# The output gate's vector-matrix product as running sums on VectorE, with TensorE adding over the partitions

## The chip, the cores and the metric

The kernel runs on one core of a Trainium2 chip. The metric is the device time of one launch, in microseconds, as the median of several runs. The engines are TensorE (PE, with PEld for its weight loads), VectorE (DVE), ScalarE (ACT), GpSimd (POOL) and SyncE (SP, which here only issues DMAs). Each engine works through its own list of instructions in a fixed order, and an instruction that waits holds up everything behind it on that engine.

## The reference

Two sequences, a prompt of 1024 tokens and a sample of 512, pass through one encoder layer with shared weights. A condition vector c (one for each sequence) gives three modulation vectors of 1024 through silu(c) @ w_ada + b_ada: shift, scale and the output gate. The layer is, cut to what matters:

```
def mod(c):  return split(silu(c) @ w_ada + b_ada, 3)     # shift, scale, gate: 1024 each
h   = rms_norm(x) * g * (1 + scale) + shift
p   = h @ w_in                                            # q, k, v, gate of both branches
o_r = bidirectional_retention(rope(q_r), rope(k_r), v_r)  # 4 heads of 128
o_a = blocked_gqa(rope(norm(q_a)), rope(norm(k_a)), v_a)  # 8 query heads, 2 key heads
y   = x + gate * (concat(o_r * silu(g_r), o_a * silu(g_a)) @ w_out)
```

The change touches one thing only: how the vector gate = silu(c) @ w_ada[:, 2048:3072] + b_ada[2048:3072] is computed for the two sequences, and where in the program that happens.

## The kernel before, in words

`sequence` runs twice: first for the sample (4 tiles of 128 tokens, first=True), then for the prompt (8 tiles). The first pass also makes shift and scale, loads and splits the weights, prepares w_out (`split_wo`) and computes the gate of both sequences. A float32 weight is split into a high and a low part (`split`: a cast on ACT, then a subtraction at line 139 on POOL for even quarters and on DVE for odd ones), and each product is three matmuls (`mm3`, lines 148 to 150).

For each retention head h the units of `head_units` project q and k (tile pqk), then v and gate (pvg). Into these, `weave` and `merge` put the steps of the head before (`ret_core`): states (psts, line 695, from vds and the rotated key ss), R0s and R1s, the decayed queries qd0s and qd1s (line 718), scores, the sum of squares sss, then m_rets and r_rets on POOL, the gated output mxs and its transpose pms. Rotation of q and k runs as rt1s (line 631) and rt2s (line 636) on DVE, and their sum ss (line 639) on POOL.

The gate comes from `gate_mod`, a generator with 16 steps. Each step loads a piece of w_ada, gr (two 128-row blocks by 256 columns, 256 KB, line 246), and issues two matmul calls with the condition vectors scT as weights (line 250, four records to a step), which add up in the PSUM banks pgm0 and pgm1. ACT copies them to gmod (line 253), and `load_gate` (line 391) adds the four column groups, the bias row and spreads the result over the partitions by a matmul with the table `sel`. `GSTEPS` says how many steps are woven into the units of heads 1, 2 and 3: 7, 7 and 3.

The pieces gr share a ring of four buffers (tag raw) with the raw quarters of all weights, for example wqks2r and wvgs2r; a DMA into the ring waits until the former content was read. The blocks of w_out (wor, line 177) go through POOL (woz, line 142), DVE (line 139) and a DMA back to HBM (wod, line 184), which POOL issues. The order of each engine's list is set by a scheduler from its own model of the times. In names, s stands for the sample, p for the prompt.

Of the kernel before, what the change touches and what calls it, by code (L numbers as in the profile page):

```python
# [11 lines left out]
F32 = mybir.dt.float32  # L12
# [3 lines left out]
ALU = mybir.AluOpType  # L16
# [3 lines left out]
P = 128  # L20
D = 1024
KD = D // P
# [22 lines left out]
def _shape_tables():  # L45
    f = np.float32
    m = np.arange(P, dtype=f)
    ident = np.eye(P, dtype=f)
    c, r = m[None, :], m[:, None]
    fwd = np.maximum(c - r, 0).astype(f)  # L50
    bwd = np.maximum(r - c, 0).astype(f)
    qf = np.broadcast_to(c + 1, (P, P))
    qb = np.broadcast_to(P - c, (P, P))
    kcol = np.ascontiguousarray(np.stack([P - 1 - m, m], 1).astype(f))
    geo = np.concatenate([fwd, bwd, qf, qb], 1).astype(f)
    sel = np.zeros((P, 2), f)
    for ct in range(4):
        for q in range(2):
            sel[32 * ct + q, q] = 1
    sel[2, :] = 1  # L60

    def rope(hd):
        half = hd // 2
        fr = (10000.0 ** (-np.arange(0, half, 2, dtype=f) / f(half))).astype(f)
        tok = np.arange(1024)
        row = (tok // GRID_W).astype(f)[:, None] * fr[None, :]
        col = (tok % GRID_W).astype(f)[:, None] * fr[None, :]
        cos = np.concatenate([np.cos(row)] * 2 + [np.cos(col)] * 2, 1)
        sin = np.concatenate([-np.sin(row), np.sin(row), -np.sin(col), np.sin(col)], 1)
        return [np.ascontiguousarray(a.astype(f).reshape(8, P, hd).transpose(1, 0, 2)) for a in (cos, sin)]  # L70

    rc, rs = rope(P)
    ac, as_ = rope(DH)
    return {"ident": ident, "geo": geo, "kcol": kcol, "sel": sel,
            "rope_rc": rc, "rope_rs": rs, "rope_ac": ac, "rope_as": as_}


# [1 line left out]
def hybrid_layer_kernel(ctx: ExitStack, tc: tile.TileContext, a: dict, y_prompt: bass.AP, y_sample: bass.AP):  # L79
    nc = tc.nc  # L80
    V, S, G, T = nc.vector, nc.scalar, nc.gpsimd, nc.tensor
# [3 lines left out]
    w_ada = a["w_ada"][0]  # L85
# [5 lines left out]
    cst = ctx.enter_context(pool("cst", bufs=1))  # L91
# [8 lines left out]
    def bank(name):  # L100
        return pcur[-1].tile([P, 512], F32, tag="bank", name=name)
# [6 lines left out]
    nc.sync.dma_start(staged, a["ident"])  # L108
    V.tensor_copy(identr, staged)
    ident = identr.bitcast(F32)  # L110
    sel = cst.tile([P, 2], F32, name="sel")
    nc.sync.dma_start(sel, a["sel"])
    mhalf = cst.tile([P, 16], F32, name="mhalf")
    V.memset(mhalf, -0.5)
    zo = cst.tile([P, 4, DH], F32R, name="zo")
# [3 lines left out]
    ones = zo[:, 2, :].bitcast(F32)  # L119
# [9 lines left out]
    scT = cst.tile([P, KD, 32], F32, name="scT")  # L129
# [5 lines left out]
    gmod = [cst.tile([P, 512], F32, name=f"gmod{n}") for n in range(2)]  # L135
# [8 lines left out]
    def ada_bias(row, c0):  # L144
        nc.sync.dma_start(row, a["b_ada"][:, c0 : c0 + 512])
# [90 lines left out]
                               op0=ALU.add, op1=ALU.add)  # L236
        V.tensor_tensor(aT[:, ks, :], md[:, n : 2 * n, :], bc(ngT[:, ks]), op=ALU.mult)

    def gate_mod(wring):
        for n in range(2):  # L240
            pm = bank(f"pgm{n}")
            for q in range(2):
                for qt in range(4):
                    raw = wring.tile([P, 2, 256], F32, tag="raw", name=f"gr{n}{q}{qt}", bufs=4)
                    c0 = 2 * D + n * 512 + q * 256
                    nc.sync.dma_start(raw, w_ada[qt * 256 : (qt + 1) * 256, c0 : c0 + 256].rearrange("(k p) c -> p k c", p=P))
                    for i in range(2):
                        k = qt * 2 + i
                        ct = k % 4
                        T.matmul(pm[32 * ct : 32 * ct + 32, q * 256 : (q + 1) * 256], scT[:, k, :], raw[:, i, :],  # L250
                                 start=(k < 4), stop=(k >= 4))
                    yield
            S.copy(gmod[n], pm)
            ada_bias(gmod[n][2:3, :], 2 * D + n * 512)

    def merge(p, n, q, m):
        done = 0
# [52 lines left out]
    def behind_ada():  # L310
        return tc.issue_after(adma[-1].ins)

    GSTEPS = {1: 7, 2: 7, 3: 3}

    def sequence(r, nt, first):
        tg = "ps"[r]
# [3 lines left out]
        with ExitStack() as sctx:  # L320
# [14 lines left out]
            kv = {}  # L335
# [52 lines left out]
            def load_gate():  # L388
                for n in range(2):
                    pgb = bank(f"pgb{tg}{n}")  # L390
                    T.matmul(pgb, sel[:, r : r + 1].broadcast_to([P, P]), gmod[n], start=True, stop=True)
                    S.copy(kv["gate"][n], pgb)

            wq = []
# [105 lines left out]
            with ExitStack() as rctx:  # L500
# [26 lines left out]
                if first:  # L527
                    with pool("st", bufs=1, reuse_waits="tile") as st:
# [8 lines left out]
                        ws, parts, i = [], [], 0  # L537
# [63 lines left out]
                def decay_tables():  # L601
                    S.activation(lg, lg, AF.Exp)
                    V.tensor_scalar_mul(lg, lg, -1.0)
                    S.activation(gd, lg, AF.Exp, scale=float(P))
                    V.memset(lns, math.log(RSCALE))
                    for h in range(RH):
                        V.tensor_scalar_mul(DT[:, h, :], geo[:, 0:P], lg[:, 0, h : h + 1])
                        V.scalar_tensor_tensor(out=DT[:, h, :], in0=geo[:, P : 2 * P], scalar=lg[:, 1, h : h + 1],
                                               in1=DT[:, h, :], op0=ALU.mult, op1=ALU.add)
                        for d in range(2):  # L610
                            S.activation(QD[:, d, h, :], geo[:, (2 + d) * P : (3 + d) * P], AF.Exp, scale=lg[:, d, h : h + 1])
                            S.activation(kd[:, d, h : h + 1], kcol[:, d : d + 1], AF.Exp, scale=lg[:, d, h : h + 1], bias=lns)
                    S.activation(DT, DT, AF.Exp, bias=lns)
# [177 lines left out]
                nsteps = 7 * ng + 1  # L791

                prev = None
                gsteps = gate_mod(wring) if first else None
                wctx = rctx.enter_context(ExitStack())
                wst = wctx.enter_context(pool(f"wst{tg}", bufs=2, reuse_waits="tile")) if first else None
                for h in range(RH + 1):
                    if h < RH:
                        sls = [slot(f"s{tg}{h}_{i}") for i in range(nt // 2)]
                        units, n = head_units(h, sls), 2 * nt  # L800
                    else:
                        wctx.close()
                        if first:
                            units, n = kvq_units(rctx.enter_context(pool(f"pa{tg}", bufs=2, reuse_waits="tile"))), 2 * nt
                        else:
                            units, n = gates(rp, "rt1"), 8 * ng
                    extra, m = itertools.islice(gsteps, GSTEPS.get(h, 0)) if first else iter(()), nsteps
                    if first:
                        m += GSTEPS.get(h, 0)
                    weave(units, n, merge(prev, nsteps, extra, m - nsteps), m + ((2, 3)[r] if h == RH else 0))  # L810
                    if h == 0:
                        decay_tables()
                    if first and h < RH:
                        for j in range(sum(WOH[:h]), sum(WOH[: h + 1])):
                            with tc.issue_after(acts["w"].ins):
                                split_wo(wst, j)
                    if h < RH:
                        prev = ret_core(h, sls)
# [318 lines left out]
```

## Time and profile before

| | |
|---|---|
| median of 3 runs (lowest, highest) | 989.43 us (989.29, 991.23) |
| span of the profiled execution | 985.3 us |
| TensorE matmul busy | 938.8 us (95%) |
| TensorE weight load busy | 813.9 us (83%) |
| VectorE busy | 626.1 us (64%) |
| ScalarE busy | 414.3 us (42%) |
| GpSimd busy | 507.7 us (52%) |

The profile is of one execution. Busy time is the time in which an engine ran an instruction. The span runs from the first to the last instruction; the measured time also has what lies around it. In a timeline each line is one instruction or several alike in a row: its start, how long it took, the engine, the line of the code, the operation, output <- inputs, shapes, and in square brackets how long the engine sat idle before it and what ended that.

### The profile page before, as it was taken

What the parts mean: (1) busy time and instruction counts of PE and PEld (TensorE: products, weight loads), DVE (VectorE), ACT (ScalarE), POOL (GpSimd) and SP (SyncE); (2) the same over time, 40 slices, a digit from 0 to 9 for tenths busy, and PEclk for the clock granted to TensorE, in tenths of its full rate; (3) what the DMA queues carried; (4) which work ended last, traced back from release to release, by engine and by line L of the source; (5) the groups of instructions that cost most, each with busy time, mean ns of one, the idle gap of its engine ahead of it and who ended that gap; (6) DMA issues with size and microseconds to landing.
All of it is one profiled execution on the core that took longest, in us unless ns stands there. A gap on an engine that the chain in (4) does not pass through costs nothing. (4 is left out here: it accounts for less than half of the span.)

```text
span 985.3 us, 15952 instructions
## 1 busy us (share of the span) xinstructions
PE 938.8 (95%) x6249; PEld 813.9 (83%) x6249; DVE 626.1 (64%) x1039; ACT 414.3 (42%) x656; POOL 507.7 (52%) x404
## 2 busy tenths in 40 slices
PE   4889998999999999999999999999979999999998
PEld 3779898987676799999999988999847776776776
DVE  2474556667886683534435243457988878978975
ACT  4252233353646652122321322241465655655562
POOL 4243544474647663122223012255899779777882
PEclk9999998999999999999999999999999999999999
DMA  9964876321911711111111112100071110111011
GB/s 274 275 191 144 269 225 218 87 78 57 382 67 44 239 50 47 41 43 44 44 35 28 26 43 70 47 7 12 1 296 68 43 44 1 44 43 45 20 43 44
DMA packets 95687, 93.02 MB, mean 94 GB/s; under 512 B 23502, under 2 KB 84858, under 8 KB 92540
## 3 DMA queue, kind: packets, MB, share of 16 engines
q1 hardware_dynamic: 92876, 77.85, 25.8%
q0 software_dynamic: 2736, 14.16, 3.6%
q8 instruction: 49, 0.80, 0.3%
q14 instruction: 26, 0.21, 0.1%
HBM read 77.30 MB, written 14.68 MB: 93 GB/s over the span
## 5 line engine op out<-in xcount | busy, mean ns | idle before, releaser
L924 POOL TENSOR_TENSOR qp<-qp,pp 128x512 f32<-128x512 f32 x96 | 159.5, 1661 | 21.3 <-ACT pp L912 15.3
L139 DVE TENSOR_TENSOR plp<-pp,php 128x1024 fp32r<-128x1024 f32 x64 | 93.6, 1464 | 19.8 <-ACT php L138 19.7
L912 ACT ACTIVATE pp<-pTp 128x1024 f32<-128x1024 f32 x64 | 65.6, 1025 | 76.8 <-PE pTp L909 40.7
L856 DVE TENSOR_REDUCE nmp<-pnp 128x1 f32<-128x1024 f32 x64 | 77.3, 1212 | 11.4 <-PE pnp L854 11.4
L138 ACT CAST php<-pp 128x1024 fp32r<-128x1024 f32 x64 | 67.2, 1051 | 16.2 <-PE pop L939 14.9
L148 PE MATMUL pvgp<-wvgp,hhp 128*128 128x256 f32 x224 | 65.1, 291 | 0.0
L148 PE MATMUL pqkp<-wqkp,hhp 128*128 128x256 f32 x224 | 64.7, 289 | 0.0
L149 PE MATMUL pvgp<-wvgp,hhp 128*128 128x256 f32 x224 | 64.4, 288 | 0.0
L150 PE MATMUL pvgp<-wvgp,hlp 128*128 128x256 f32 x224 | 63.9, 285 | 0.0
L150 PE MATMUL pqkp<-wqkp,hlp 128*128 128x256 f32 x224 | 63.7, 284 | 0.0
L149 PE MATMUL pqkp<-wqkp,hhp 128*128 128x256 f32 x224 | 63.4, 283 | 0.0
L940 PE MATMUL pop<-plp,VVp 128*128 128x512 f32 x128 | 52.1, 407 | 5.7 <-DVE plp L139 5.6
L148 PE MATMUL pyp<-wo,Mhp 128*128 128x512 f32 (+1 forms) x136 | 52.8, 389 | 1.2 <-DVE op L951 0.7
L150 PE MATMUL pyp<-wo,Mlp 128*128 128x512 f32 (+1 forms) x136 | 51.6, 382 | 0.5 <-DVE Mlp L139 0.5
L149 PE MATMUL pyp<-wo,Mhp 128*128 128x512 f32 (+1 forms) x136 | 51.9, 382 | 0.0
L639 POOL TENSOR_TENSOR sp<-rt1p,rt2p 128x512 f32<-128x512 f32 x16 | 22.5, 1405 | 56.4 <-DVE rt2p L636 56.4
L939 PE MATMUL pop<-php,VVp 128*128 128x512 f32 x128 | 51.0, 398 | 0.3 <-ACT php L138 0.3
L124 POOL TENSOR_SCALAR m_retp<-ssp 128x4 f32<-128x4 f32 x8 | 1.6, 195 | 89.6 <-DVE ssp L745 89.4
L897 PE MATMUL pTp<-Q1Tp,kkp 128*128 128x512 f32 x128 | 41.4, 404 | 3.6 <-ACT pp L912 2.9
L148 PEld LDWEIGHTS pqkp<-wqkp,hhp 128*128 128x128 f32 x224 | 43.0, 192 | 0.0
L149 PEld LDWEIGHTS pqkp<-wqkp,hhp 128*128 128x128 f32 x224 | 43.0, 192 | 0.0
L150 PEld LDWEIGHTS pqkp<-wqkp,hlp 128*128 128x128 f32 x224 | 42.9, 192 | 0.0
(465 smaller groups left out, 3120.7 us busy)
## 6 DMA issues: line engine op xcount, KB each, us to landing
wo<-wod SPq DMA_DIRECT2D x16, 1024.0 KB, 5.8
wa<-in_w_ada_dram SPq DMA_DIRECT2D x16, 512.0 KB, 6.4
wod<-woz POOLq DMA_DIRECT2D x8, 1024.0 KB, 6.0
gr<-in_w_ada_dram SPq DMA_DIRECT2D x16, 256.0 KB, 4.8
xn<-in_x_prompt_dram SPq DMA_DIRECT2D x8, 512.0 KB
xrp<-in_x_prompt_dram SPq DMA_DIRECT2D x8, 512.0 KB, 3.4
out_dram<-xrp POOLq DMA_DIRECT2D x7, 512.0 KB, 3.0
xs<-in_x_sample_dram SPq DMA_DIRECT2D x4, 512.0 KB, 6.1
```

The source lines that it names most:

```text
L138: hi_eng(hi, src)
L139: lo_eng.tensor_tensor(lo, src, hi.bitcast(F32), op=ALU.subtract)
L148: T.matmul(out, lh, rh, start=first, stop=False)
L149: T.matmul(out, lh, rl, start=False, stop=False)
L150: T.matmul(out, ll, rh, start=False, stop=last)
L639: G.tensor_tensor(qk, t1, t2, op=ALU.add)
L856: V.tensor_reduce(nm[:, h : h + 1], pn[:, :ntok], AX.X, ALU.max, negate=True)
L897: T.matmul(pT[:, i * 512 : (i + 1) * 512], kk[v][:, kb], st8[t]["Q1T"][:, hs, :].rearrange("p h q -> p (h q)"), start=True, stop=False)
L912: S.activation(p, pT, AF.Exp)
L924: G.tensor_tensor(acc, acc, p[:, i * 512 : (i + 1) * 512], op=ALU.add)
L939: T.matmul(po, lv, ph[:, c], start=(kb == 0), stop=False)
L940: T.matmul(po, lv, pl[:, c], start=False, stop=(kb == nt - 1))
```

## The change

`gate_mod` no longer uses TensorE. `gate_start`, called after head 0's units, clears four 128x512 accumulators with POOL (gmod0 and gmod1 for the prompt, the two tiles kv["gate"], called gates in the lists, for the sample) and loads the bias into their row 0 by four DMAs. Each of the 16 steps loads one 128-row block by 512 columns (again 256 KB) and runs two scalar_tensor_tensor instructions on DVE, one for each sequence: accumulator = block * scT + accumulator, with one scalar to a partition. That makes 32 instructions on 128x512 float32 with both inputs in SBUF. `load_gate` then adds over the 128 partitions with the same number of matmuls as before, with a column of ones in place of `sel`, whose table and load are gone. Head 3 gets 2 steps in place of 3.

```diff
-    def gate_mod(wring):
-        for n in range(2):
-            pm = bank(f"pgm{n}")
-            for q in range(2):
-                for qt in range(4):
-                    raw = wring.tile([P, 2, 256], F32, tag="raw", name=f"gr{n}{q}{qt}", bufs=4)
-                    c0 = 2 * D + n * 512 + q * 256
-                    nc.sync.dma_start(raw, w_ada[qt * 256 : (qt + 1) * 256, c0 : c0 + 256].rearrange("(k p) c -> p k c", p=P))
-                    for i in range(2):
-                        k = qt * 2 + i
-                        ct = k % 4
-                        T.matmul(pm[32 * ct : 32 * ct + 32, q * 256 : (q + 1) * 256], scT[:, k, :], raw[:, i, :],
-                                 start=(k < 4), stop=(k >= 4))
-                    yield
-            S.copy(gmod[n], pm)
-            ada_bias(gmod[n][2:3, :], 2 * D + n * 512)
+    def gate_start(accs):
+        for acc in accs:
+            for n in range(2):
+                G.memset(acc[n], 0.0)
+                ada_bias(acc[n][0:1, :], 2 * D + n * 512)
+
+    def gate_mod(wring, accs):
+        for k in range(KD):
+            for n in range(2):
+                raw = wring.tile([P, 512], F32, tag="raw", name=f"gr{n}{k}", bufs=4)
+                c0 = 2 * D + n * 512
+                nc.sync.dma_start(raw, w_ada[k * P : (k + 1) * P, c0 : c0 + 512])
+                for r, acc in enumerate(accs):
+                    V.scalar_tensor_tensor(out=acc[n], in0=raw, scalar=scT[:, k, r : r + 1], in1=acc[n], op0=ALU.mult, op1=ALU.add)
+                yield
...
-    GSTEPS = {1: 7, 2: 7, 3: 3}
+    GSTEPS = {1: 7, 2: 7, 3: 2}
...
-                    T.matmul(pgb, sel[:, r : r + 1].broadcast_to([P, P]), gmod[n], start=True, stop=True)
+                    T.matmul(pgb, ones[:, 0:1].broadcast_to([P, P]), kv["gate"][n], start=True, stop=True)
...
-                gsteps = gate_mod(wring) if first else None
+                gsteps = gate_mod(wring, (gmod, kv["gate"])) if first else None
...
+                        if first:
+                            gate_start((gmod, kv["gate"]))
```

The scheduler's lists differ in the stretch from about 20 to 200 us; behind it they are alike but for line numbers. In the lists below a name ends in the numbers of its buffer and its tile: gr00 is row block 0 of half 0 (the digits are half, then block).

DVE's list at the end of the last normalised tile (hls) and the first rotation of head 0 (rt1s, rt2s), before:

```order
L139 TENSOR_TENSOR wvgs1_840<-wvgs1r1_846,wvgs1_840 128x2x256
L511 TENSOR_SCALAR hfs0_7_542<-xTs0_7_536,aT_81,shT_80 128x512
L513 TENSOR_TENSOR hls0_98<-hfs0_7_542,hhs0_97 128x512
L139 TENSOR_TENSOR wvgs1_840<-wvgs1r3_856,wvgs1_840 128x2x256
L631 TENSOR_TENSOR rt1s0_0_762<-p0s0_0_186,rc_738 128x2x128 x2
L636 TENSOR_TENSOR rt2s0_0_763<-p0s0_0_186,rs_740 128x128 x4
```

The same place on DVE after:

```order
L132 TENSOR_TENSOR wvgs1_846<-wvgs1r1_852,wvgs1_846 128x2x256
L230 TENSOR_TENSOR aT_79<-md7_529,ngT_80 128x2
L503 TENSOR_SCALAR hfs0_7_540<-xTs0_7_534,aT_79,shT_78 128x512
L132 TENSOR_TENSOR wvgs1_846<-wvgs1r3_862,wvgs1_846 128x2x256
L505 TENSOR_TENSOR hls0_96<-hfs0_7_540,hhs0_95 128x512
L245 SCALAR_TENSOR_TENSOR gmod0_82<-gr00_897,scT_76,gmod0_82 128x512
L245 SCALAR_TENSOR_TENSOR gates0_109<-gr00_897,scT_76,gates0_109 128x512
L245 SCALAR_TENSOR_TENSOR gmod1_83<-gr10_944,scT_76,gmod1_83 128x512
L245 SCALAR_TENSOR_TENSOR gates1_110<-gr10_944,scT_76,gates1_110 128x512
L245 SCALAR_TENSOR_TENSOR gmod0_82<-gr01_980,scT_76,gmod0_82 128x512
L245 SCALAR_TENSOR_TENSOR gates0_109<-gr01_980,scT_76,gates0_109 128x512
L623 TENSOR_TENSOR rt1s0_0_760<-p0s0_0_184,rc_736 128x2x128 x2
```

Six of the new instructions, on three pieces, now stand ahead of the first rt1s, and two more stand between rt1s and rt2s.

POOL's list at the same time, from the last split of head 1's weights to the first rotated key (ss), before:

```order
L139 TENSOR_TENSOR wvgs1_840<-wvgs1r2_851,wvgs1_840 128x2x256 [waits DMAHW7_49,DMAHW0_49,Activation_49]
L639 TENSOR_TENSOR ss0_0_760<-rt1s0_0_762,rt2s0_0_763 128x512 [waits DVE_49,PE_49]
L142 TENSOR_SCALAR woz0_1191<-wor0_1189 128x2x512 [waits DMAHW1_49,DMAHW7_49,PE_49,Pool_49]
L639 TENSOR_TENSOR ss0_1_761<-rt1s0_1_771,rt2s0_1_772 128x512 [waits DVE_49]
L184 DMA wod0_60<-woz0_1191 128x2048 [waits DVE_49]
```

And after:

```order
L132 TENSOR_TENSOR wvgs1_846<-wvgs1r2_857,wvgs1_846 128x2x256 [waits DMAHW3_49,DMAHW2_49,Activation_49]
L135 TENSOR_SCALAR woz0_1196<-wor0_1194 128x2x512 [waits DMAHW4_49,PE_49,Pool_49]
L631 TENSOR_TENSOR ss0_0_758<-rt1s0_0_760,rt2s0_0_761 128x512 [waits DVE_49]
L177 DMA wod0_60<-woz0_1196 128x2048 [waits DVE_49]
L631 TENSOR_TENSOR ss0_1_759<-rt1s0_1_769,rt2s0_1_770 128x512 [waits DVE_49]
```

The block of w_out, which waits for a DMA, has changed places with the first ss. In SP's list the load of that block (wor0) stood behind four pieces gr before, and stands behind six after; the fifth and the sixth wait for a ring buffer that DVE's new instructions give back.

DVE's list at head 0's sum of squares and output, before:

```order
L362 SCALAR_TENSOR_TENSOR ss1_0_817<-tg_s1_0_1095,pvgs1_0_1034 128x256
L745 TENSOR_REDUCE sss0_0_1111<-sqs0_0_1109 128x4
L750 SCALAR_TENSOR_TENSOR mxs0_0_1117<-pos0_0_1098,r_rets0_0_1115,ss0_0_760 128x128 x2
L750 SCALAR_TENSOR_TENSOR mxs0_0_1117<-pos0_0_1098,r_rets0_0_1115,ss0_1_761 128x128 x2
L362 SCALAR_TENSOR_TENSOR ss1_1_818<-tg_s1_1_1180,pvgs1_1_1126 128x256
```

And after:

```order
L354 SCALAR_TENSOR_TENSOR ss1_0_823<-tg_s1_0_1100,pvgs1_0_1039 128x256
L132 TENSOR_TENSOR woz1_1573<-wor1_1571,woz1_1573 128x2x512
L132 TENSOR_TENSOR woz2_1580<-wor2_1577,woz2_1580 128x2x512
L737 TENSOR_REDUCE sss0_0_1116<-sqs0_0_1114 128x4
L742 SCALAR_TENSOR_TENSOR mxs0_0_1122<-pos0_0_1103,r_rets0_0_1120,ss0_0_758 128x128 x2
```

Two splits of w_out blocks now stand ahead of the sum of squares; on POOL their copies and both wod DMAs stand ahead of m_rets and r_rets in the same way. At head 1's sum of squares one such split (woz4) has moved ahead of mxs.

## Rows read from the trace of the kernel before

**Rows 1.** The page's first part: busy us, share of the span, instructions.

```profile
PE 938.8 (95%) x6249; PEld 813.9 (83%) x6249; DVE 626.1 (64%) x1039; ACT 414.3 (42%) x656; POOL 507.7 (52%) x404
```

**Rows 2.** All that touches tile gr: durations, then idle us and times, landing.

```profile
L250 PE MATMUL pgm<-gr,scT x64: 376/380/404, 65.9 to 143.9; 128*32 128x256 f32 x64
...
  DMA gr<-in_w_ada_dram: 6.4, 7
...
  PE pgm L250: 3.3, 4
...
DMA to landing us min/median/max: 2.7/4.8/7.8
```

**Rows 3.** Timeline of PE from 65 to 74 us.

```profile
65.66 0.27 PE L150 MATMUL pqks<-wqks,hls 128*128 128x256 f32 x1
65.87 0.63 PE L250 MATMUL pgm<-gr,scT 128*32 128x256 f32 x4
...
66.64 0.28 PE L149 MATMUL pqks<-wqks,hhs 128*128 128x256 f32 x1
...
69.28 0.28 PE L150 MATMUL pqks<-wqks,hls 128*128 128x256 f32 x1
...
71.37 0.63 PE L250 MATMUL pgm<-gr,scT 128*32 128x256 f32 x4 [0.83 <-DMA gr<-in_w_ada_dram]
73.00 0.63 PE L250 MATMUL pgm<-gr,scT 128*32 128x256 f32 x4 [1.00 <-DMA gr<-in_w_ada_dram]
73.55 0.71 PE L695 MATMUL psts<-vds,ss 128*128 128x128 f32 x4
```

**Rows 4.** Timeline of DVE from 60 to 69 us.

```profile
60.42 0.69 DVE L139 TENSOR_TENSOR wvgs<-wvgs1r,wvgs 128x512 fp32r<-128x512 f32 x1 [0.93 <-ACT wvgs L138]
...
62.02 1.48 DVE L513 TENSOR_TENSOR hls<-hfs,hhs 128x512 fp32r<-128x512 f32 x1
...
64.33 0.76 DVE L631 TENSOR_TENSOR rt1s<-p0s,rc 128x256 f32<-128x256 f32 x2 [0.23 <-PE p0s L150]
65.00 0.87 DVE L636 TENSOR_TENSOR rt2s<-p0s,rs 128x128 f32<-128x128 f32 x4
...
68.02 1.13 DVE L608 SCALAR_TENSOR_TENSOR DT<-geo,lg,DT 128x128 f32<-128x128 f32 x4
```

**Rows 5.** Timelines of DVE and of POOL at 351 us, in the prompt.

```profile
351.63 1.91 DVE L608 SCALAR_TENSOR_TENSOR DT<-geo,lg,DT 128x128 f32<-128x128 f32 x4
...
351.41 1.20 POOL L298 TENSOR_SCALAR xn<-xn,r_x 128x1024 f32<-128x1024 f32 x1
```

**Rows 6.** Timeline of SP's DMA issues from 59 to 66 us.

```profile
59.30 5.19 SPq L246 DMA_DIRECT2D gr<-in_w_ada_dram  x4
65.74 0.37 SPq L177 DMA_DIRECT2D wor<-in_w_out_dram  x1
```

**Rows 7.** Timeline of POOL from 66 to 101 us.

```profile
66.01 1.28 POOL L639 TENSOR_TENSOR ss<-rt1s,rt2s 128x512 f32<-128x512 f32 x1 [3.06 <-DVE lns L605]
70.81 1.04 POOL L142 TENSOR_SCALAR woz<-wor 128x1024 fp32r<-128x1024 f32 x1 [3.52 <-DMA wor<-in_w_out_dram]
...
93.79 0.19 POOL L124 TENSOR_SCALAR m_rets<-sss 128x4 f32<-128x4 f32 x1 [7.84 <-DVE sss L745]
...
100.68 1.05 POOL L142 TENSOR_SCALAR woz<-wor 128x1024 fp32r<-128x1024 f32 x1 [5.58 <-DMA wor<-in_w_out_dram]
```

**Rows 8.** Timeline of PE at head 0's first transposed output.

```profile
96.99 0.27 PE L503 MATMUL pms<-identr,mxs 128*128 128x128 f32 x1
```

**Rows 9.** Timeline of PE around 158 us.

```profile
157.70 0.80 PE L741 MATMUL pos<-R1s,qd1s 128*128 128x128 f32 x2 [2.89 <-DVE qd1s L718]
```

**Rows 10.** Windows of 3 us: length, busy us (instructions) by engine, PE clock, DMA.

```profile
160.00:163.00 3.00, 3.00 (x16) 3.00 (x16) 0.31 (x1) 0.00 (x0) 0.60 (x1) 0.50 0.84 308
163.00:166.00 3.00, 3.00 (x24) 3.00 (x24) 0.46 (x1) 0.60 (x1) 0.00 (x0) 0.87 0.50 203
166.00:169.00 3.00, 3.00 (x27) 3.00 (x26) 1.64 (x7) 0.26 (x1) 1.23 (x2) 1.00 0.16 46
```

More of the change, by code (lines that the diff above doesn't have):

```diff
@@ L55, in _shape_tables @@
     geo = np.concatenate([fwd, bwd, qf, qb], 1).astype(f)
-    sel = np.zeros((P, 2), f)
-    for ct in range(4):
-        for q in range(2):
-            sel[32 * ct + q, q] = 1
-    sel[2, :] = 1
     def rope(hd):
@@ L73, in _shape_tables @@
     ac, as_ = rope(DH)
-    return {"ident": ident, "geo": geo, "kcol": kcol, "sel": sel,
+    return {"ident": ident, "geo": geo, "kcol": kcol,
             "rope_rc": rc, "rope_rs": rs, "rope_ac": ac, "rope_as": as_}
@@ L110, in hybrid_layer_kernel @@
     ident = identr.bitcast(F32)
-    sel = cst.tile([P, 2], F32, name="sel")
-    nc.sync.dma_start(sel, a["sel"])
     mhalf = cst.tile([P, 16], F32, name="mhalf")
@@ L237, in ada_part @@
         V.tensor_tensor(aT[:, ks, :], md[:, n : 2 * n, :], bc(ngT[:, ks]), op=ALU.mult)
-    def gate_mod(wring):
-        for n in range(2):
-            pm = bank(f"pgm{n}")
-            for q in range(2):
-                for qt in range(4):
-                    raw = wring.tile([P, 2, 256], F32, tag="raw", name=f"gr{n}{q}{qt}", bufs=4)
-                    c0 = 2 * D + n * 512 + q * 256
-                    nc.sync.dma_start(raw, w_ada[qt * 256 : (qt + 1) * 256, c0 : c0 + 256].rearrange("(k p) c -> p k c", p=P))
-                    for i in range(2):
-                        k = qt * 2 + i
-                        ct = k % 4
-                        T.matmul(pm[32 * ct : 32 * ct + 32, q * 256 : (q + 1) * 256], scT[:, k, :], raw[:, i, :],
-                                 start=(k < 4), stop=(k >= 4))
-                    yield
-            S.copy(gmod[n], pm)
-            ada_bias(gmod[n][2:3, :], 2 * D + n * 512)
+    def gate_start(accs):
[12 more added lines that the diff above has]
+                yield
     def merge(p, n, q, m):
```

## The prediction

> **What bounds the kernel now.** I read the busy times first: TensorE is busy for 938.8 of the 985.3 us of the profiled span, VectorE for 626.1 [rows 1]. So TensorE is the bound on the whole, and any work taken off it should shorten the kernel, unless TensorE then waits in the place where that work stood. Next I read the rows of the tile gr, to see what the gate's product costs TensorE: 64 records between 65.9 and 144 us, and waits for the pieces' DMAs, of which 3.3 us in four waits stand on the matmuls themselves [rows 2]. The timelines of TensorE, VectorE, GpSimd and of SP's issues in that stretch then say what stands around those pieces. The prompt's pass runs in the same order before and after, so the whole answer lies before 200 us.
>
> **What is removed.** Each of the 16 pieces is four records. A lone one between projection matmuls starts at 65.87; the second projection matmul behind it starts at 66.64, where it would have stood at 65.90 (65.66 plus two steps of 0.12), which is 0.74 us [rows 3]. Five pieces stand in a row after 69.28: without them psts could start at 69.40, with them it starts at 73.55, so 4.15 us, 1.83 of it waits for DMA (0.83 and 1.00) [rows 3]. The ten others at 0.75 are 7.5, and the rest of their waits is 3.3 − 1.83 = 1.4. Together 0.74 + 4.15 + 7.5 + 1.4 = 13.8 us. That is the most that TensorE gives back: 10.5 us of work and 3.3 of waits. ACT's two copies cost nothing on the path.
>
> **What is added.** VectorE gets 32 scalar_tensor_tensor on 128x512 float32, both inputs in SBUF. No row before shows that form at that size. The nearest is the subtraction of line 139, also two float32 inputs in SBUF, 128x512: 0.69 us at 60.42, and back to back such instructions start 0.60 apart, which I take; 32 make 19 us. The lower end is the same; the upper one comes from the four small ones of line 608 (128x128): 1.13 us together, so 0.28 each, and four times the elements is 1.13 [rows 4]. So 19 to 36 us on an engine that is idle for a third of the time, but not in the stretch 60 to 75 us, where its timeline is nearly full.
>
> Beside a GpSimd instruction that reads SBUF the same four of line 608 took 1.91 us in place of 1.13, the time to GpSimd's end plus their own [rows 4, 5]. The Trainium skill ("SBUF — State Buffer", section "SBUF: two separate sides") states why: VectorE instructions with two SBUF inputs and GpSimd share a pair of ports as an exclusive lock, and whichever starts first blocks the other for its whole length. It speaks against this change, since all 32 are of that form; it is a rival below.
>
> The four clears run on GpSimd while it is idle early on; four bias loads against one table less are about 0.5 us more on SP's queue, at a place where the weights' loads follow. I take +0.5 and allow −0.5 to +1.5.
>
> **What is moved, place one (61 to 76 us).** In the new lists six gate instructions stand ahead of head 0's rt1s, two more ahead of rt2s, and the first block of w_out stands on GpSimd ahead of the first ss. Times here are in the old run's clock. The first piece may be loaded when VectorE has split the second quarter of head 1's weights, 60.42 + 0.69 = 61.1 [rows 4]; a piece takes 4.8 us in the median (2.7 to 7.8) [rows 2], so it lands at 66.0. By then hls is done (63.5 before, some 0.5 later now) and VectorE stands still with rt1s queued behind the pieces, which before ran at 64.33 [rows 4]. Six instructions end at 69.6, rt1s at 70.3, two more at 71.5, rt2s at 72.3, against 65.87 before. The fifth and sixth piece wait for ring buffers that the first two pieces' instructions free, at 67.3 and 68.5; the w_out block is queued behind them on SP, so it is asked for at about 69.0 instead of 65.74 [rows 6]. Before, from that issue to its copy on GpSimd went 70.81 − 65.74 = 5.1 us [rows 6, 7]. So woz runs at 74.1 to 75.1, and ss, 1.28 us [rows 7], ends at 76.4. The first psts needs ss: it starts at 76.4 in place of 73.55, though TensorE arrives there at 69.1 (73.55 − 4.15 − 0.74 + 0.45). It waits 7.3 us.
>
> A wait of 2.89 us at 157.70 was followed by a granted clock of 0.50 (1.2 GHz), 16 matmuls in 3 us instead of 27, then 24 in the next 3 us at 0.87 [rows 9, 10]. That is about 2.5 us lost. A wait of 7.3 us should do the same. So place one costs 76.4 − 73.55 + 2.5 = **+5.4 us**, where its six pieces should have given 4.9.
>
> **Place two (93 to 120 us).** One lone piece fewer: −0.75, so 4.65 late at 97. Now head 0's sss and mxs stand behind two w_out splits on VectorE, and m_rets behind two copies and two DMA issues on GpSimd; before, m_rets ran at 93.79 and the copy only at 100.68, when its block had landed, and TensorE took pms at 96.99 without a wait [rows 7, 8]. The block is asked for right behind head 1's last weight load, which no longer waits for a piece on TensorE; I estimate that issue at 92.5, landing with the 5.1 us of above at 97.7. Two copies, two splits, the DMA issues, sss and the chain to mxs take it to about 103.8. TensorE arrives at 101.6: wait 2.2, if the block landed as late as before 5 more. Then five pieces fall away (3.75 and the 1.4 of waits: 5.2), while VectorE has 14 gate instructions there, each pair behind a DMA, in front of the rotations and the states; I put the wait that this leaves at 1.4 us, with 0 and 5 as ends. Sum: −0.75 + 2.2 − 5.2 + 1.4 = **−2.3**.
>
> **Place three (125 to 165 us).** Four lone pieces: −3.0. Head 1's mxs is behind a w_out split that before came later; by the same reckoning it is 3.8 us late (0 to 6 with the clock). The old wait of 2.89 us at 157.70 [rows 9] and its slow clock shrink when TensorE comes later; I take half of the wait, −1.5 (0 to −5.4). Sum **−0.7**.
>
> **Sum.** 0.5 + 5.4 − 2.3 − 0.7 = +2.9 us on the profiled span: 988.2. The span stands 4.1 us under the median of the runs (989.43 − 985.3), which I leave: 992.3 us. A measurement of this kernel can tell about 0.2% (2 us) from no change, so +2.9 is a small loss.
>
> **Rivals.**
> First, TensorE keeps its gain: −13.8 + 0.5 gives 976.1. For it speaks that TensorE waited rarely in 69 to 150 us other than for gr, so that VectorE was ahead; against it that the first ss cannot come before the first piece has landed, whatever else is true. In a half-way case the first pieces land in the lower end of 2.7 us [rows 2] and the w_out block with them: place one is then 4 us earlier and keeps its clock (−6.5), and the total is −3.6, 986. It decides at a landing of about 3.3 us.
> Second, waits just cancel the gain: within 2 us of 989.4. This needs place one at +3 rather than +5.4, for which a quicker landing by 2 us would do.
> Third, the port lock: each gate instruction is held like those of line 608 [rows 4, 5], 1.0 us in place of 0.60. In place one eight such stand on the path, +3.3 us; with 14 more in place two +4 to 5 of which half shows. That would give 997 to 998. Against it, GpSimd is idle for 3.06 and 3.52 us ahead of its instructions in place one [rows 7], so little stands beside the first eight.
> Fourth, that the product does not leave TensorE at all is excluded: no piece is left in its list.
>
> **How the numbers follow.** The forecast (a loss over 2 us, without the lock) 0.42; with the lock 0.08; cancelled 0.18; some or all of the gain kept 0.32, of which nearly the whole 13 us 0.10. The range leaves out the full gain and the far end of clock drops in all three places: 979 to 999. Its lower end takes in the half-way case with place two at its lower end; its upper end the lock. The forecast's own range, by the bounds of the waits, is 991.5 to 999.
>
> **What would show it.** Right: TensorE's first psts after a wait of several us put down to ss or vds, its clock at 0.50 behind; VectorE idle before the first gate instruction with DMA gr as the releaser; woz ahead of the first ss on GpSimd; the gate instructions at 0.6 to 0.7 us. Step two is right if pms of head 0 waits for mxs. Wrong: no wait of TensorE over 2 us between 66 and 80 us, pieces landing under 3.3 us, or gate instructions at over 1 us with GpSimd busy beside them. The 14 instructions in place two are wrong if R1s and qd1s come without a wait.

## The result and the profile after

The changed kernel takes 996.51 us (median of four runs, 996.01 to 998.02) where before takes 989.36: 1.0079 times as long, with a 95% interval of 1.0052 to 1.0106 (the two medians alone stand at 1.0072). The forecast was a loss, 992.3 us; the loss is there and is 7.2 us rather than 2.9.

The first line of the page of after shows where one would look first: TensorE's busy time hardly fell (938.8 before, [rows 1]), although 64 records of it are gone, and VectorE has 19.3 us more.

```profile
PE 937.9 (94%) x6185; PEld 818.9 (82%) x6185; DVE 645.4 (65%) x1071; ACT 413.6 (42%) x654; POOL 513.8 (52%) x408
```

What took the place of the pieces of [rows 2, 3] is seen in all that touches the tile gr in after: the two kinds of new instruction, then what VectorE waited for, then the landing times.

```profile
L245 DVE SCALAR_TENSOR_TENSOR gmod<-gr,scT,gmod x16: 735/740/1589, 67.7 to 158.7; 128x512 f32<-128x512 f32 x16
L245 DVE SCALAR_TENSOR_TENSOR gates<-gr,scT,gates x16: 735/742/1776, 68.4 to 159.3; 128x512 f32<-128x512 f32 x16
...
  DMA gr<-in_w_ada_dram: 1.2, 1
...
DMA to landing us min/median/max: 2.9/3.8/4.4
```

An instruction takes 0.74 us, and two of the 32 far more (1.59 and 1.78). VectorE waited for a piece only once, for 1.2 us, so it did not stand still for the first piece, as the prediction had it in place one. The load that does come late there is that of the w_out block behind the pieces on SP: GpSimd stands 10.21 us for it, with the first rotated key (ss) queued behind.

```profile
74.99 1.04 POOL L135 TENSOR_SCALAR woz<-wor 128x1024 fp32r<-128x1024 f32 x1 [10.21 <-DMA wor<-in_w_out_dram]
76.00 1.26 POOL L631 TENSOR_TENSOR ss<-rt1s,rt2s 128x512 f32<-128x512 f32 x1
```

Where the time went is read from TensorE's timeline. These are its waits of over 2 us between 35 and 180 us in after, with the scores of heads 0 and 1 and the output of head 2 for comparison:

```profile
40.10 0.58 PE L141 MATMUL p0s<-wqks,hhs 128*128 128x256 f32 x1 [3.97 <-ACT hhs L501]
...
65.72 0.39 PE L141 MATMUL p0s<-wqks,hhs 128*128 128x256 f32 x1 [2.63 <-ACT hhs L501]
...
78.01 1.19 PE L687 MATMUL psts<-vds,ss 128*128 128x128 f32 x4 [4.06 <-ACT vds L671]
...
93.47 1.05 PE L717 MATMUL pscs<-qTs,kTs 128*128 128x128 f32 x8
...
109.67 0.47 PE L495 MATMUL pms<-identr,mxs 128*128 128x128 f32 x1 [6.22 <-DVE mxs L742]
...
129.04 1.05 PE L717 MATMUL pscs<-qTs,kTs 128*128 128x128 f32 x8
...
145.56 0.47 PE L495 MATMUL pms<-identr,mxs 128*128 128x128 f32 x1 [4.68 <-DVE mxs L742]
...
176.06 0.33 PE L495 MATMUL pms<-identr,mxs 128*128 128x128 f32 x1 [0.26 <-DVE mxs L742]
```

The same instructions in before, of which the prediction showed two others ([rows 3, 8]):

```profile
38.60 0.39 PE L148 MATMUL p0s<-wqks,hhs 128*128 128x256 f32 x1 [2.11 <-ACT hhs L509]
...
61.12 0.39 PE L148 MATMUL p0s<-wqks,hhs 128*128 128x256 f32 x1 [1.04 <-ACT hhs L509]
...
86.06 1.06 PE L725 MATMUL pscs<-qTs,kTs 128*128 128x128 f32 x8
...
118.37 1.06 PE L725 MATMUL pscs<-qTs,kTs 128*128 128x128 f32 x8
...
132.35 0.27 PE L503 MATMUL pms<-identr,mxs 128*128 128x128 f32 x1
...
168.54 0.27 PE L503 MATMUL pms<-identr,mxs 128*128 128x128 f32 x1
```

Set side by side, after is late by 1.5 us at the first line, by 4.6 at the second (65.72 − 61.12), by 4.5 at the first psts, 12.7 at head 0's pms, 13.2 at head 1's and 7.5 at head 2's. From there on both run the same list; another microsecond or so is lost near 228 us, and the spans end 8.6 us apart (993.9 and 985.3). That is more than the 7.2 us between the medians: the run of after with this span took 996.01 us, 2.1 more than its span, and by the same 2.1 the profiled execution of before, with 985.3, was some 2 us quicker than the median of before (an estimate). So TensorE is 4.6 us late before the first gate instruction, some 8 us more are lost between 78 and 110 us, and 5.7 us come back between 146 and 176, where the old wait of [rows 9] is gone.

Behind each long wait the clock fell. The windows of after at 40 and at 110 us (columns as in [rows 10]) show it: the granted clock is 0.50, and at 110 us there are 16 matmuls in 3 us where [rows 10] has 27 at 1.00.

```profile
40.00:43.00 3.00, 2.90 (x13) 2.74 (x13) 1.94 (x5) 0.31 (x2) 0.00 (x0) 0.50 1.11 289
...
110.00:113.00 3.00, 3.00 (x16) 3.00 (x16) 1.92 (x5) 0.00 (x0) 1.32 (x2) 0.50 0.99 415
```

What stood ahead of head 0's pms is in the timelines of VectorE and GpSimd. GpSimd stands 9.20 us for a block of w_out, VectorE 7.13 us for GpSimd's copy, and the sum of squares, which TensorE needs, is queued behind two such splits; m_rets follows at 107.92 (before: at 93.79, ahead of these copies, [rows 7]).

```profile
103.63 1.22 DVE L132 TENSOR_TENSOR woz<-wor,woz 128x1024 fp32r<-128x1024 f32 x1 [7.13 <-POOL woz L135]
105.79 1.22 DVE L132 TENSOR_TENSOR woz<-wor,woz 128x1024 fp32r<-128x1024 f32 x1 [0.94 <-POOL woz L135]
106.93 0.68 DVE L737 TENSOR_REDUCE sss<-sqs 128x4 f32<-128x512 f32 x1
...
102.55 1.04 POOL L135 TENSOR_SCALAR woz<-wor 128x1024 fp32r<-128x1024 f32 x1 [9.20 <-DMA wor<-in_w_out_dram]
```

### The profile page after: what moved, and what is told of

It is laid out like the page before. It is cut to its first block, busy times and chain, and to the rows that moved or that the text cites. A ratio compares the mean times of both kernels' runs of the same rounds, so it can differ in the third digit from the quotient of the medians.

```text
span 993.9 us, 15868 instructions
## 1 busy us (share of the span) xinstructions
PE 937.9 (94%) x6185; PEld 818.9 (82%) x6185; DVE 645.4 (65%) x1071; ACT 413.6 (42%) x654; POOL 513.8 (52%) x408
## 5 line engine op out<-in xcount | busy, mean ns | idle before, releaser
L850 DVE TENSOR_REDUCE nmp<-pnp 128x1 f32<-128x1024 f32 x64 | 77.3, 1212 | 10.7 <-PE pnp L848 10.7
L141 PEld LDWEIGHTS pvgp<-wvgp,hhp 128*128 128x128 f32 x224 | 42.9, 192 | 0.0
```

The costliest lines, as they stand in the source:

```text
L141: T.matmul(out, lh, rh, start=first, stop=False)
L850: V.tensor_reduce(nm[:, h : h + 1], pn[:, :ntok], AX.X, ALU.max, negate=True)
```

## The experiments

Two theories were set against each other. **Q**: the loss is made by what stands in line behind something else in an engine's list (bias loads on SP, w_out blocks ahead of mxs, gate instructions ahead of rt1s and R1s). **L**: the loss is VectorE's load, 32 instructions and their exclusion with GpSimd, wherever they stand. Ratios below are to the kernel before, measured beside each run on the same chip, where its median was 987.0 to 988.0 us. Where the 95% intervals of two ratios overlap, their difference is not clear of noise.

### e1: the bias loads later

```diff
-                            gate_start((gmod, kv["gate"]))
+                            with behind_ada():
+                                gate_start((gmod, kv["gate"]))
```

> The changed kernel with one edit: the four bias loads are issued behind the last load of w_ada for shift and scale, not in the middle of the start-up loads (in the changed kernel they stand on SP at 29 us, and TensorE's wait for the normalised tile at 40.10 is 3.97 us against 2.11 before, with a slow clock behind it). Theory Q (the loss comes from instructions that stand in line behind others, the bias loads on SP being one such place): the wait at 40 us goes back to about 2 us, the clock stays at 1.00 there, and the time falls by 2 to 4.5 us, to 992 to 994.5. Rival L (the loss is the load of the 32 new instructions on VectorE, from 67 us on): the start-up gets its time back, but the later waits for psts and pms grow by as much, so 996 to 997.

Measured: 993.58 us, ratio 1.0054 (1.0035 to 1.0073), where after has 1.0079. TensorE's timeline:

```profile
37.78 0.39 PE L141 MATMUL p0s<-wqks,hhs 128*128 128x256 f32 x1 [1.45 <-ACT hhs L501]
...
76.92 1.22 PE L687 MATMUL psts<-vds,ss 128*128 128x128 f32 x4 [6.54 <-POOL ss L631]
```

The wait of 3.97 us is 1.45, and by the ratios 2.5 us of the loss are gone, inside Q's range; the intervals of e1 and after overlap, so the size of that gain is not shown as firmly as the wait. But the first psts waits 6.54 us now, so part of what the start gained was only waited for later: the matmul that stands at 65.72 in after comes 2.8 us earlier, psts only 1.1. What it waits for is ss, behind the w_out block on GpSimd; TensorE's and GpSimd's timelines of e1:

```profile
62.88 0.28 PE L141 MATMUL p0s<-wqks,hhs 128*128 128x256 f32 x1
...
73.63 1.59 POOL L135 TENSOR_SCALAR woz<-wor 128x1024 fp32r<-128x1024 f32 x1 [9.01 <-DMA wor<-in_w_out_dram]
75.19 1.69 POOL L631 TENSOR_TENSOR ss<-rt1s,rt2s 128x512 f32<-128x512 f32 x1
```

This is the prediction's place one nearly to the number: it had woz at 74.1, the end of ss and psts at 76.4, and a wait of 7.3 us.

### e2, e3 and e4: the old order put back

e2 holds the w_out blocks behind mxs and r_rets of the head two before, e3 holds the gate instructions behind both rotations of head 0 (and the first w_out block behind the second ss), e4 has e1, e2 and e3 and puts aT ahead of the splits of wvgs1.

```diff
+                                if h >= 2:
+                                    nm = f"{tg}{h - 2}_0"
+                                    after.enter_context(tc.issue_after(acts[f"ret{nm}"].ins))
+                                    after.enter_context(tc.issue_after(acts[f"mx{nm}"].ins))
...
+                with tc.issue_after(acts["rts0_1"].ins):
                     for r, acc in enumerate(accs):
```

> The changed kernel with one edit: the w_out blocks 1 to 3 are split behind head 0's mxs and r_rets, and 4 to 7 behind head 1's, as their order was before. Theory Q: TensorE's waits of 6.22 and 4.68 us for mxs, at 109.7 and 145.6, go, and the slow clock behind each (some 2.5 us each); of the 16 us a part is lost again at the older wait for qd1s: 983 to 989. Rival L: VectorE is late with or without these blocks, pms still waits over 3 us in at least one head, 993 to 997.

> The changed kernel with one edit: the gate instructions stand behind both rotations of head 0 (rt2s of its second half) on VectorE, and the first w_out block behind the second ss on GpSimd. Theory Q: TensorE's wait of 4.06 us for the first psts falls under 2.5 us and the clock behind it stays; but the ring's buffers come free later, so the waits for pms at heads 0 and 1 stay as they are: 991 to 995. Rival L: the pile of gate instructions only moves, psts or R0s wait as long: 996 to 999.

> The three edits together, and a fourth: aT of the last normalised tile stands ahead of the splits of head 1's second weight on VectorE, as it did before. The 32 instructions are all still there. Theory Q: no wait of TensorE over 2.5 us from 60 to 165 us; the product's 10 to 13.8 us come through: 976 to 982. Rival L: 988 or more, since the 32 instructions (21 us at 0.66) delay the rotations and states of each head in any order. Rival S (a start-up effect that has nothing to do with order): 990 to 994.

Measured: e2 990.93 us, 1.0028 (1.0003 to 1.0053); e3 996.62 us, 1.0081 (1.0047 to 1.0116); e4 993.91 us, 1.0042 (1.0023 to 1.0060). In e2 the waits for mxs are gone, as Q has it, and most of the loss with them, but less than Q's range; e2 lies between the ranges of Q and L, and a wait of 5.52 us for head 1's R1s is new (at 131.62). e3 gave nothing, as L has it. e4 missed Q's 976 to 982 by far, and so Q in that simple form fell; its time fits L, and S as well, but its start is not late (psts at 74.16 beside 73.55 before). Its timelines of TensorE and then VectorE show why:

```profile
94.39 0.77 PE L734 MATMUL pos<-R1s,qd1s 128*128 128x128 f32 x2 [5.42 <-DVE R1s L694]
...
86.36 0.28 DVE L692 COPY R1s<-psts 128x128 f32<-128x128 f32 x1
86.56 0.74 DVE L246 SCALAR_TENSOR_TENSOR gates<-gr,scT,gates 128x512 f32<-128x512 f32 x1
...
93.91 0.34 DVE L694 SCALAR_TENSOR_TENSOR R1s<-R1s,gd,psts 128x128 f32<-128x128 f32 x1
```

The gate instructions that were held behind the rotations now lie between the steps of R0s and R1s, one or two ahead of each; the last R1s ends at 94.2, and TensorE waits 5.42 us for it. The time had only moved.

### e5 and e6: the pieces in other buffers, at other places

Both load whole row blocks (1024 columns) into buffers of their own and hand them out in heads 2 and 3. e5 has the order mended (e1, e2, aT) and holds four blocks behind head 0's mxs and four behind head 1's; e6 has no other edit.

```diff
+            raw = slot(f"gr{k}")
+            nc.sync.dma_start(raw, w_ada[k * P : (k + 1) * P, 2 * D : 3 * D])
+            with tc.issue_after(acts[f"mxs{k // 4}_0"].ins):
...
-    GSTEPS = {1: 7, 2: 7, 3: 2}
+    GSTEPS = {2: 4, 3: 4}
```

> The 32 gate instructions at other places. As in the run before (late bias loads, w_out blocks behind mxs, aT first), but the pieces have buffers of their own (slots of 1024 columns, one row block each) instead of the weights' ring, and four row blocks stand behind head 0's mxs, four behind head 1's, on VectorE: no gate instruction stands ahead of a head's rt1s, R0s or R1s any more. Theory Q (what costs is what stands behind the gate's instructions in VectorE's list): waits for R1s of 5.4 and 3.7 us in the last run go, no wait of TensorE over 2.5 us from 66 to 160 us, 975 to 983. Rival L (32 instructions of 0.66 us and their exclusion with GpSimd make VectorE late wherever they stand): waits of 3 us or more return at sTs, mxs or qd1s: 986 to 993.

> The changed kernel with the pieces in buffers of their own and handed out later (none in head 1's units, four row blocks each in head 2's and 3's), and nothing else: bias loads, w_out blocks and aT as the scheduler puts them. Theory Q: place one is free of gate instructions, so the first psts waits under 2.5 us; whether head 0's and head 1's mxs wait depends on where the w_out blocks fall: 980 to 992. Rival L: 990 to 996.

Measured: e5 995.48 us, 1.0072 (1.0052 to 1.0093); e6 999.83 us, 1.0122 (1.0095 to 1.0148). e5 up to head 1 does what Q says: first psts at 72.23, head 0's pms at 96.38 without a wait. Both are slower than both theories' ranges. In e5 twelve gate instructions then pile up among head 2's scores and ahead of its sss:

```profile
170.76 0.47 PE L495 MATMUL pms<-identr,mxs 128*128 128x128 f32 x1 [6.78 <-DVE mxs L742]
```

That is L's price at an ill-chosen place. e6 shows the start and the w_out blocks with it (p0s waits 4.11 us, pms 3.99 and 7.33).

### e7, e8, e11: how much is VectorE's time

e7 leaves out the sample's sums (16 of 32 instructions), e8 the loads and all 32, e11 keeps all loads and instructions but on one column.

```diff
-                for r, acc in enumerate(accs):
+                for r, acc in enumerate(accs[:1]):
...
-                    V.scalar_tensor_tensor(out=acc[n], in0=raw, scalar=scT[:, k, r : r + 1], in1=acc[n], op0=ALU.mult, op1=ALU.add)
+                    V.scalar_tensor_tensor(out=acc[n][:, 0:1], in0=raw[:, 0:1], scalar=scT[:, k, r : r + 1], in1=acc[n][:, 0:1], op0=ALU.mult, op1=ALU.add)
```

> The changed kernel without the running sums of the sample (16 of the 32 instructions; that part of the computation is left out). DMAs and all else are kept. Rival L: half of the load gone, half or more of the loss gone, 986 to 991. Theory Q: what stands behind DMAs stays behind them (bias loads, w_out blocks ahead of mxs); the first place gets 4 instructions or 2.7 us quicker: 991 to 996.

> The changed kernel without the gate's product at all: no piece is loaded and none of the 32 instructions is there; the clears, the bias loads and load_gate stay (the product is left out of the result). It is what taking the product off TensorE gives if VectorE's part were free. By the sum of the rows it gives 13.8 us less the start-up's bias loads (2 to 4): 976 to 980. If TensorE waits for VectorE or for the weights anyway, less: 980 to 986. If it is no faster than before, TensorE was never the bound in this stretch.

> The changed kernel with each of the 32 gate instructions on one column in place of 512 (the sums of the other columns are left out): the same loads, the same waits for them, the same w_out blocks ahead of mxs, but 0.1 us in place of 0.66. If the loss is what stands behind the loads and the w_out blocks (theory Q), 994 to 997 where before is 987 to 989. If it is VectorE's time (rival L), as e8: 987 to 990.

Measured: e8 987.61 us, **1.0002** (0.9986 to 1.0019); e11 991.69, 1.0033 (1.0013 to 1.0053); e7 991.89, 1.0054 (1.0035 to 1.0073); after 1.0079. So with the product off TensorE and nothing put on VectorE the kernel is as fast as before: of the 13.8 us of [rows 2, 3] nothing is left in the time. From e8 to e11 (the loads and their places in the lists) it rises by 0.3%, from e11 to after (VectorE's time) by 0.46%. The intervals of e8 and after lie clear of each other, but e11's touches both, so the two parts are not settled one by one; e7 can't be told from e11 or from after. e7 fits Q, e11 lies between the two ranges.

Where the gain went in e8 is seen in TensorE's timeline: there is no gate instruction in this kernel, and waits stand where after has them.

```profile
41.08 0.58 PE L141 MATMUL p0s<-wqks,hhs 128*128 128x256 f32 x1 [3.95 <-ACT hhs L496]
...
76.21 0.68 PE L682 MATMUL psts<-vds,ss 128*128 128x128 f32 x4 [2.86 <-ACT vds L666]
...
105.74 0.48 PE L490 MATMUL pms<-identr,mxs 128*128 128x128 f32 x1 [5.24 <-DVE mxs L737]
```

### e9, e10 and e12: the order mended, without and with the product

e9 is e8 with the order mended as in e5 (e1, e2, aT; not e3's edges). e10 is the whole change with that order, the buffers of e5, and one row block behind head 0's mxs, one behind head 1's scores, two behind head 1's mxs and four behind head 2's. e12 also puts the splits of head 3's first weight behind head 1's qd1s.

```diff
+    GANCH = ['mxs0_0', 'sTs1_0', 'mxs1_0', 'mxs1_0', 'mxs2_0', 'mxs2_0', 'mxs2_0', 'mxs2_0']
...
+            with tc.issue_after(acts[GANCH[k]].ins):
...
+    GSTEPS = {2: 1, 3: 3, 4: 4}
...
+                            with tc.issue_after(acts["qd1s1_0"].ins) if first and h == 3 else ExitStack():
+                                w = load_w(wring, f"wqk{tg}{h}", [(h * P, P), (512 + h * P, P)])
```

> No gate product at all, as in the run e8 (no piece loaded, no running sum; left out of the result), with the order mended as in e4 (late bias loads, w_out blocks behind mxs, aT first). In e8 TensorE lost nothing to the product and still took as long as before, with waits of 4.0 us at the start, 2.9 for the first psts and 5.2 and 3.2 for mxs. Theory O (the order of the lists ate what TensorE gave back): with the order mended 13.8 us less the 2.9 us wait for the first psts come through, 976 to 980 where before is 987. Rival F (the pieces only filled gaps in which TensorE waits for the states, the scores and the tables anyway): waits of that size turn up at qd1s or mxs instead, 983 to 987.

> The whole change at places of free VectorE time: order mended as in e4, the pieces in buffers of their own, one row block behind head 0's mxs, one behind head 1's scores, two behind head 1's mxs and four behind head 2's. Theory O: the first psts at about 72 us, pms of heads 0 and 1 without a wait over 2 us; two row blocks stand beside head 2's scores and may cost 3 us there: 979 to 985 where before is 987. Rival L (32 instructions cost wherever they stand): 988 to 993.

> The run e10 with one more edit: the splits of head 3's first weight stand behind head 1's decayed queries (qd1s) on VectorE. In e10 one of them took 3.86 us at 114.58, held by three GpSimd instructions one after the other (114.13 to 117.89), with qd0s and qd1s behind it, and TensorE waited 2.60 us at 119.79 and then ran at the slow clock. Theory: that wait goes under 1 us and the clock stays at 1.00: 3 to 5 us less than e10, 978 to 980 beside 988 of before (ratio 0.990 to 0.992). Rival: the split falls on the scores instead (sTs), TensorE waits there, no change: ratio 0.994 to 0.997.

Measured: e9 974.62 us, **0.9870** (0.9833 to 0.9908); e10 982.75, 0.9953 (0.9932 to 0.9974); e12 980.25, **0.9930** (0.9913 to 0.9948). Theory O held against F: with the order mended some 13 us do come through when the product costs nothing, and e12, which computes all, beats both kernels: before by 0.7% (7 us), after by some 15 us. Between e9 and e12 lie 0.6%, some 6 us, which is what the loads and the 32 instructions cost at better places. e5 and e10 have the same order edits and the same buffers, and differ in the edits only by the places of the product's loads and instructions: 1.0072 against 0.9953.

The 13 us of e9 are not the 13.8 of [rows 2, 3] one for one. In TensorE's timeline of e9, 7.0 us are gained by head 1's pms (132.35 before) and 14.0 by head 2's (168.54 before):

```profile
74.02 0.68 PE L682 MATMUL psts<-vds,ss 128*128 128x128 f32 x4 [2.86 <-ACT vds L666]
...
125.40 0.27 PE L490 MATMUL pms<-identr,mxs 128*128 128x128 f32 x1
...
154.52 0.33 PE L490 MATMUL pms<-identr,mxs 128*128 128x128 f32 x1 [0.21 <-DVE mxs L737]
```

Between these two lies the wait of 2.89 us of before [rows 9] with the slow clock behind it, and e9 has neither. Why they are gone was not tried.

e10's weak place, which e12 was made for, shows in the timelines of TensorE, VectorE and GpSimd: one split is held through three GpSimd instructions, and qd1s stands behind it.

```profile
119.79 0.74 PE L735 MATMUL pos<-R1s,qd1s 128*128 128x128 f32 x2 [2.60 <-DVE qd1s L712]
...
114.58 3.86 DVE L132 TENSOR_TENSOR wqks<-wqks3r,wqks 128x512 fp32r<-128x512 f32 x1
...
114.13 1.28 POOL L132 TENSOR_TENSOR wqks<-wqks3r,wqks 128x512 fp32r<-128x512 f32 x1
115.37 1.29 POOL L633 TENSOR_TENSOR ss<-rt1s,rt2s 128x512 f32<-128x512 f32 x1
116.63 1.26 POOL L132 TENSOR_TENSOR wqks<-wqks3r,wqks 128x512 fp32r<-128x512 f32 x1
```

In e12 this wait is gone and TensorE stands 1.20 us for sTs instead, whose turn comes behind the moved splits. The ratio lies between the two expectations, and its interval overlaps e10's, so what this one edit gave is not settled.

Not tried: the order edits of e10 and e12 on the kernel before, with the product left on TensorE. How much of the 0.7% the old product would have got by the new order alone is therefore open.

## Why the prediction was right, and where its steps were off

**The sign and the kind of cause** were right: waits of TensorE for instructions that the new lists put behind others, and a slow clock behind the waits. The 64 records removed were worth nothing net in these lists (e8). That the time came out inside the range was in part luck. At head 2's pms the sum said +2.9 and 7.5 was measured, and that hides larger errors that partly cancel: 4.1 too little at the start, 2.6 too much in place one, 5.6 too little in place two and 2.5 too little given back in place three. The measured 996.51 us lies nearer to the 997 to 998 of the rival with the lock than to the forecast of 992.3, but the trace does not bear that rival out (below).

**The start-up** was mis-sized: +0.5 was said, with 1.5 as the upper end, and 4.6 us it was at 65.72. The four bias loads cost more than their issue: SP's later loads moved by some 2.5 us, TensorE's wait grew from 2.11 to 3.97, and the clock fell to 0.50 behind it. aT, which the prediction did not price by itself, adds to it: in after it stands behind a split, and VectorE's timeline (the last line below is GpSimd's) shows its input md done at 60.55, the split waiting for its cast until 62.48, and aT at 63.58, taking 1.21 us for two elements to a partition (0.16 in before). It ends at 64.79, within 0.02 us of GpSimd's split beside it.

```profile
60.40 0.15 DVE L228 SCALAR_TENSOR_TENSOR md<-md,bT 128x2 f32<-128x2 f32 x1
62.48 1.18 DVE L132 TENSOR_TENSOR wvgs<-wvgs1r,wvgs 128x512 fp32r<-128x512 f32 x1 [1.92 <-ACT wvgs L131]
63.58 1.21 DVE L230 TENSOR_TENSOR aT<-md,ngT 128x2 f32<-128x2 f32 x1
...
63.38 1.39 POOL L132 TENSOR_TENSOR wvgs<-wvgs1r,wvgs 128x512 fp32r<-128x512 f32 x1 [0.28 <-ACT wvgs L131]
```

e1, which moves the bias loads alone, is 2.5 us nearer to before by the ratios.

**Place one** was right in its mechanism, and its price can be read only where the start is not late. In after the lateness grows by 2.8 us from 65.72 to head 0's scores (93.47 in after, 86.06 before: 7.4), not by 5.4. Since hls itself was late, the first piece had landed by then, and VectorE did not wait for it; rt1s came behind six gate instructions at 0.66 apart. The w_out block was late as said, and ss behind it ended at 77.26. The named releaser of psts is ACT's vds, which starts at 77.37 and needs ss and the tables kd. ACT's chain runs through VectorE too: the constant lns (a memset of 0.06 us, before at 65.8) stands behind rt2s in VectorE's list, and the first kd waits for it; the seven others end at 77.46. So two chains end within 0.2 us of each other, and the prediction had one of them. In e1, with the earlier start, psts is 3.4 us late (2.9 said, before the clock) and waits for ss itself. The step that failed is to add the two terms: TensorE waits at psts for a chain that hangs on loads, so lateness that it brings there is largely swallowed (2.8 us less at the start gave 1.1 at psts). First VectorE, then ACT in after:

```profile
74.49 0.06 DVE L597 MEMSET lns<- 128x1 f32 x1
...
74.60 0.39 ACT L604 ACTIVATE kd<-kcol,lns,lg 128x1 f32<-128x1 f32 x1 [1.10 <-DVE lns L597]
...
77.37 1.70 ACT L671 ACTIVATE vds<-ss,kd 128x256 f32<-128x256 f32 x4
```

And a floor was missed: even with nothing in the way (e8, e9) the first psts waits 2.86 us for vds. So of the 4.15 us of the five pieces in [rows 3] some 2.9 stood in a wait that TensorE would have had anyway. In the sum of 13.8 us this part was never to be had.

**Place two** was the term with the largest error: it was said to give back 2.3 us and cost 3.3 (lateness 7.4 at head 0's scores, 129.04 − 118.37 = 10.7 at head 1's). The mechanism, sss behind two w_out blocks, was right, and its price was not: the copy of the block began at 102.55, where the prediction had the block landed at 97.7 (before, the copy began at 100.68), the wait was 6.22 us in place of 2.2 ("if the block landed as late as before 5 more" was the end that came true), and the slow clock behind it was not in the sum. R1s and qd1s came without a wait, so the 1.4 us put there were none. **Place three** held its mechanism as well: head 1's mxs was waited for 4.68 us (3.8 said), and the old wait of 2.89 us at 157.70 [rows 9] vanished altogether. With 3.2 us back in place of 0.7 the sum at head 2's pms is 4.6 + 2.8 + 3.3 − 3.2 = 7.5.

**The price of an instruction** was 0.66 from start to start, 0.74 alone, against 0.60. The 2.5 us for a fall of the clock is 1.6 by the two windows of [rows 10] (16 and 24 matmuls where 27 fit in 3 us); the stretch from 157.70 to 160, also at 0.50, brings it to some 2.7. The 1.91 us of line 608 in [rows 5] are 0.2 less than the time to GpSimd's end (0.98) and the 1.13 of its own. Beside GpSimd a gate instruction takes up to 1.78, as in these two lines of VectorE and GpSimd in after:

```profile
84.55 1.78 DVE L245 SCALAR_TENSOR_TENSOR gates<-gr,scT,gates 128x512 f32<-128x512 f32 x1
...
84.05 1.72 POOL L631 TENSOR_TENSOR ss<-rt1s,rt2s 128x512 f32<-128x512 f32 x1 [1.61 <-DVE rt2s L628]
```

It ends 0.56 us after GpSimd's, which ended at 85.77: as if most of it ran only then. That is the lock which the Trainium skill ("SBUF — State Buffer", section "SBUF: two separate sides") states for VectorE instructions with two SBUF inputs: the trace agrees, with 1.78 beside and 0.74 alone. But two of the 32 took over 1 us (the medians stay at 0.74), so as a price of the gate instructions that rival decided little. Other instructions of VectorE were held as well: aT above, on TensorE's path to 65.72, and e10's split of 3.86 us.

Left open: the microsecond near 228 us, in lists that are alike, was not tried; all changed kernels here but e10 and e12 have it (e8 and e9 too, which have no gate instruction). The scheduler chose a new list for each edit, so that e7, e8 and e11 also differ from after in places other than the edit; the split of the loss into 0.3 and 0.46% carries that uncertainty on top of the noise.

## What to carry to other kernels

Work taken off the busiest engine is worth its time only where that engine would not have waited at that place anyway: take it out without putting it anywhere else (e8) and see, before its time is counted as a gain. A null result of such a test does not say that the engine was never the bound: in another order the same removal gave 13 us (e9). Work put on an engine with free time costs by what stands behind it in that engine's list, so choose its place by the free stretches and the chains that the bound engine waits for (e5's 1.0072 and e10's 0.9953 are the same instructions in other places), and see that a scheduler has not also changed the order of things that the change did not touch.

## What the runs showed of the hardware

A wait of TensorE of nearly the same length was followed by the slow clock in one run and not in another: 2.86 us before 74.02 in e9, with a granted clock of 1.00 (2.4 GHz) behind it, and 2.87 us before 73.16 in e12, with 0.55 (mostly 1.2 GHz). The first psts waits 2.86 or 2.87 us in eight kernels: the clock behind it stayed at 1.00 in e3, e4, e9 and e10, and fell in e5, e6, e8 and e12. The windows of e9, and then of e12:

```profile
75.00:78.00 3.00, 3.00 (x28) 3.00 (x27) 2.93 (x10) 0.69 (x2) 1.44 (x2) 1.00 0.21 87
```

```profile
75.00:78.00 3.00, 3.00 (x17) 3.00 (x17) 1.44 (x7) 0.00 (x0) 2.01 (x2) 0.55 0.61 257
```

So 2.5 us for a wait of that length is not a fixed price: it came in four of these eight profiles. What decides it was not tried.
